# Feed-forward with features on partitions, and one group of small products for each expert

## The chip, the cores and the metric

The kernel runs on one core of a Trainium2 chip. The metric is the device time of one execution in microseconds, the median over several runs. TensorE is called PE here, VectorE DVE, ScalarE ACT, GpSimd POOL, SyncE SP, as in the profile.

## The reference

Two blocks of two layers each follow each other on 256 tokens of 1024 features, all in float32.

```python
# first block, for each of 2 layers
x = x + 0.5 * swiglu(rms_norm(x, ffn1_norm[l]), ffn1_w_gate[l], ffn1_w_up[l], ffn1_w_down[l])
x = x + mixing(rms_norm(x, mix_norm[l]))          # three kinds of attention, w_in, w_out
x = x + 0.5 * swiglu(rms_norm(x, ffn2_norm[l]), ffn2_w_gate[l], ffn2_w_up[l], ffn2_w_down[l])

def swiglu(x, w_gate, w_up, w_down):              # 1024 x 2816, 1024 x 2816, 2816 x 1024
    return (jax.nn.silu(x @ w_gate) * (x @ w_up)) @ w_down

# second block, for each of 2 layers
x = layer_norm(alpha * x + gated_linear_attention_and_sgu(x))
x = layer_norm(alpha * x + attention_to_memory(x, mem))
x = layer_norm(alpha * x + grouped_moe(x))

# grouped_moe: a router picks 2 experts of one group of 4 for each token
for e in range(16):
    h = jax.nn.silu(xt @ w_gate[e]) * (xt @ w_up[e])   # 1024 x 512 each
    y = y + gate[:, e:e + 1] * (h @ w_down[e])         # 512 x 1024
```

## The kernel before

**Weights.** All weights pass once through SBUF in units of 512 KB (`UNIT`, 128 partitions x 1024 floats), in the order of use. `load_ahead` (L261) issues their loads on SP's queue as soon as one of a number of rooms is free. Products that need full precision split each unit into a high and a low part: `whi` on ACT (L310), `wlo` on DVE (L284), and `mm3` (L356) makes three matmuls of one product, high by high, low by high, high by low. The experts take their units whole, in plain float32.

**Feed-forward.** `gated` (L515) goes through the 2816 features in the chunks of `CUTS`, of 512 and once of 256. In a chunk, `into` multiplies the 256 tokens, as two stationary tiles of 128 (`NH` halves h, tiles `xt`), with the gate weights that stream past them (bank `mm`), then with the up weights (bank `tp`); DVE makes the product (L609). Between the two stands the down product of the chunk before it (`accA`, `accB`). Down needs features on partitions, so PE turns the product in 128 x 128 transposes (L558, with `ident`), two units behind the start of the next chunk's gate, and ACT and DVE split it (L561, L562). `last_down` finishes one token half after the other, and as each of the four banks is done, `renew` adds it to `x` (L633), and the next stage's `xt` is made: transposes on PE (`transpose4`, L432), high part on ACT (L443), low part on DVE (L445), a square on ACT (L462) for the norm.

**Between.** The constants of the mixing stage are made in steps that `gated` calls at the start of chunks; their small products take banks of the kind `mm` (L169, L697, L714).

**Experts.** Each expert has 64 places. Four experts are gathered at once: `gather(q)` multiplies the tokens `xn` with the 0/1 matrix `pick` (L1834, 4 steps of 8 matmuls into a bank `tp`, copied to `xg`). `into(e)` (L1925) multiplies 64 gathered rows with gate and up, the two at once in the two column halves of the array; `turn(e)` transposes the result (L1939), ACT and DVE make the product (L1941, L1942), `down(e)` (L1950) multiplies with the down weights. `way_back(e)` turns the gated places (L1856, from `pk`, which POOL makes at L1851), and `scatter(e)` (L1966) adds the result to the tokens' banks `ys`, with 64 rows of the array. The order is written out: behind the first of `into(e + 1)`'s four pairs of units stands `turn(e)`, behind the third `scatter(e - 1)`; `way_back(e + 1)` and the steps of a gather are generators that count ticks. There are three banks `mm` and one `tp`.

**Memory.** In layer 0 the experts' stage also loads and turns the memory's tokens for layer 1 (`stage`, L1354).

Of the kernel before, what the change touches and what calls it, by code (L numbers as in the profile page):

```python
# [45 lines left out]
CUTS = [512, 256, 512, 512, 512, 512]  # L46
# [23 lines left out]
def the_kernel(  # L70
# [90 lines left out]
    def columns(c0, n, pool, *loads):  # L161

        rows = pool.tile([n, P], FT, name=f"rows{c0}") if pool else t2()[:n, :P]
        for r0, f0, t in loads:
            nc.sync.dma_start(rows[r0:r0 + t.shape[0], f0:f0 + t.shape[1]], t)

        def put():
            pt = bank("mm")[:, :n]
# [95 lines left out]
    def load_ahead(upto=None):  # L264
# [250 lines left out]
    def gated(xt, ready, chunks, scale, factor, last=True, renew=None, between={}, up="tp"):  # L515
# [3 lines left out]
        ys = []  # L519

        def into(tag, halves, hooks, done):
            W = Taken()
            o = [bank(tag)[:, :W.n] for _ in range(NH)]
            if halves == "start":

# [13 lines left out]
            order = [(h, u) for h in range(NH) for u in range(W.count)] if halves else \  # L539
                [(h, u) for u in range(W.count) for h in range(NH)]  # L540
            for i, (h, u) in enumerate(order):
                for k in W.ks(u):
                    mm3(o[h], *xt.at(h, k), *W(k), k == 0, k == KD - 1)
                if h:
                    W.close(1)
                if u == W.count - 1:
                    done(h, o[h])
                tick()
                for at, f in hooks:
                    if at == i + 1:  # L550
                        f()

        def turned(h, u, n):

            tp = tbank()
            nf = n // P
            for f in range(nf):
                nc.tensor.transpose(tp[:, f], u[:, f * P:(f + 1) * P], ident)  # L558
            uh = t2(FR).rearrange("p (f t) -> p f t", t=P)
            ul = t2(FR).rearrange("p (f t) -> p f t", t=P)  # L560
            nc.scalar.activation(uh[:, :nf], tp[:, :nf], AF.Copy)  # L561
            nc.vector.tensor_sub(ul[:, :nf], tp[:, :nf], uh[:, :nf].bitcast(FT))  # L562
            return uh, ul

        def down(c, ut):
            W = Taken()
            if not ys:
                ys.extend([bank(ACC[h]) for _ in range(2)] for h in range(NH))
            for f in range(W.kt):
                for h in range(NH):  # L570
                    for j in range(2):
                        mm3(ys[h][j], *(t[:, f] for t in ut[h]), *W(f, j), c == 0 and f == 0, False)
# [4 lines left out]
        def last_down(c, ut, gs):  # L577
            W = Taken()
            if not ys:
                ys.extend([bank(ACC[h]) for _ in range(2)] for h in range(NH))  # L580
            for h in range(NH):
                for j in range(2):
                    for f in range(W.kt):
                        mm3(ys[h][j], *(t[:, f] for t in ut[h]), *W(f, j), c == 0 and f == 0, last and f == W.kt - 1)
                        if (h, j) == (1, 1):
                            W.close(1)
                        if h == j == 0 and f == 1:
                            ut[1] = turned(1, late[1], late[2])
                        if f == W.kt - 1 and renew:
                            gs[h].append(spawn(renew(h, j, ys[h][j])))  # L590
                        if f % 2:
                            tick()

        ut, u, gs, late = {}, [None, None], [[], []], [None] * 3
        for c in range(chunks):
            if c in between:
                between[c]()
            hooks = []
            if c:
                n0 = u[0].shape[-1]  # L600
                hooks = [(2, lambda: ut.update({h: turned(h, u[h], n0) for h in range(NH)}))]
            ss = [None, None]

            def silu(h, o):
                ss[h] = t2()[:, :o.shape[-1]]
                nc.scalar.activation(ss[h], o, AF.Silu, scale=scale(h))

            def product(h, o):
                nc.vector.scalar_tensor_tensor(ss[h], o, factor(h), ss[h], op0=OP.mult, op1=OP.mult)  # L609

            into("mm", "start" if c == 0 else None, hooks, silu)
            n = ss[0].shape[-1]
            if c:
                down(c - 1, ut)
                ut = {}

            if c < chunks - 1:
                into(up, None, [], product)
            else:
                cnt = 8 * n // UNIT  # L620
                into(up, "up", [(cnt + max(1, cnt // 2), lambda: ut.update({0: turned(0, ss[0], n)}))], product)
                late[1:] = [ss[1], n]
            u = ss
        last_down(chunks - 1, ut, gs)
        return ys, gs

    def ffn(xt, rs, ready, start, between={}):

        nxt = start()
        r = lambda h: rs[h][:, 0:1]  # L630
# [1480 lines left out]
```

## Time and profile before

| | us |
|---|---|
| median of 3 runs (lowest, highest) | 2193.13 (2188.81, 2196.97) |
| profiled execution | 2191.49 |
| its span | 2189.8 |
| PE busy in the span | 2117.0 (97%) |
| DVE, ACT, POOL busy | 1118.9, 892.4, 172.5 |
| mean DMA rate | 224 GB/s |

The span goes from the first to the last instruction; the profiled execution has 1.7 us around it. Four feed-forwards take about 204, 204, 190 and 205 us, two mixing stages 221 and 217, the second block's layers about 510 and 430, of which the experts' stages take 282 (from 1478 to 1760, with the memory's keys at their end) and 224. The ends of a matmul are modelled, so that the times from one start to the next are what counts for a stream of them. TensorE's granted clock is 0.995 of full in the mean.

### The profile page before, as it was taken

How to read it: one execution, taken by the hardware profiler on the slowest of the kernel's cores; microseconds unless marked ns; L12 is line 12 of the kernel's file. 1: busy time of each engine (PE TensorE's matmuls, PEld its weight loads, DVE VectorE, ACT ScalarE, POOL GpSimd, SP SyncE). 2: the span in 40 equal slices, each digit the busy share in tenths (PEclk: the TensorE clock that was granted, in tenths of full speed). 3: DMA queues.
4: the chain of work that ended last, by engine and by line, in shares of the span. 5: the costliest groups of instructions: out<-in, count | busy, mean ns of one | idle time of the engine just before them, and what ended most of it. 6: DMA issues, size and time to landing. Idle time of an engine off the chain costs nothing. (4 is left out here: it accounts for less than half of the span.)

```text
span 2189.8 us, 29392 instructions
## 1 busy us (share of the span) xinstructions
PE 2117.0 (97%) x11117; PEld 1554.0 (71%) x11117; DVE 1118.9 (51%) x1999; ACT 892.4 (41%) x1424; POOL 172.5 (8%) x231
## 2 busy tenths in 40 slices
PE   8999999999999999999999999989999999989997
PEld 6778878788888888787888887963333677953332
DVE  6445787554555547866554547651111558341112
ACT  5444555454444446554544454521111454421111
POOL 1000100100000002102000002011000111010000
PEclk9999999999999999999999999999999999999999
DMA  7554643556556655535756555679998936589996
GB/s 250 187 181 149 211 145 111 178 177 200 174 172 193 196 159 171 187 98 173 242 183 190 158 170 198 207 258 338 393 394 297 360 116 236 178 313 383 394 393 247
DMA packets 240076, 490.48 MB, mean 224 GB/s; under 512 B 17539, under 2 KB 44851, under 8 KB 239923
## 3 DMA queue, kind: packets, MB, share of 16 engines
q1 hardware_dynamic: 239634, 487.42, 65.9%
q8 instruction: 92, 1.51, 0.3%
q10 hardware_dynamic: 288, 1.05, 0.1%
q14 instruction: 62, 0.50, 0.1%
HBM read 487.34 MB, written 1.07 MB: 223 GB/s over the span
## 5 line engine op out<-in xcount | busy, mean ns | idle before, releaser
L284 DVE TENSOR_TENSOR wlo<-raw,whi 128x1024 fp32r<-128x1024 f32 (+1 forms) x508 | 614.7, 1228 | 292.7 <-ACT whi L310 288.3
L310 ACT ACTIVATE whi<-raw 128x1024 fp32r<-128x1024 f32 (+1 forms) x508 | 525.1, 1052 | 293.3 <-PE tp L359 115.7
L1925 PE MATMUL mm<-raw,xg 128*64 128x512 f32 x1024 | 243.7, 604 | 7.7 <-PEq L1981 7.0
L357 PE MATMUL accB<-whi,xt 128*128 128x512 f32 (+3 forms) x448 | 176.2, 393 | 0.0
L359 PE MATMUL accB<-whi,xt 128*128 128x512 f32 (+3 forms) x448 | 165.5, 369 | 0.0
L358 PE MATMUL accB<-wlo,xt 128*128 128x512 f32 (+3 forms) x448 | 165.3, 369 | 0.0
L1925 PEld LDWEIGHTS mm<-raw,xg 128*64 128x64 f32 x1024 | 69.8, 137 | 133.5 <-issue 123.0
L357 PE MATMUL tp<-whi,xt 128*128 128x512 f32 (+1 forms) x384 | 143.8, 374 | 0.0
L359 PE MATMUL tp<-whi,xt 128*128 128x512 f32 (+1 forms) x384 | 143.4, 373 | 0.0
L358 PE MATMUL tp<-wlo,xt 128*128 128x512 f32 (+1 forms) x384 | 142.5, 371 | 0.0
L357 PE MATMUL mm<-whi,xt 128*128 128x512 f32 (+1 forms) x320 | 121.2, 379 | 1.4 <-DVE nbias L715 0.7
L359 PE MATMUL mm<-whi,xt 128*128 128x512 f32 (+1 forms) x320 | 118.3, 370 | 0.0
L358 PE MATMUL mm<-wlo,xt 128*128 128x512 f32 (+1 forms) x320 | 117.6, 368 | 0.0
L1950 PE MATMUL mm<-raw,t 128*64 128x512 f32 x512 | 117.3, 599 | 0.0
L1930 ACT ACTIVATE t<-mm 128x512 f32<-128x512 f32 x32 | 19.1, 597 | 188.4 <-PE mm L1925 188.4
L359 PEld LDWEIGHTS accB<-whi,xt 128*128 128x128 f32 x448 | 84.1, 188 | 15.1
L357 PEld LDWEIGHTS accB<-whi,xt 128*128 128x128 f32 x448 | 84.5, 189 | 13.3 <-issue 1.0
L358 PEld LDWEIGHTS accB<-wlo,xt 128*128 128x128 f32 x448 | 84.5, 189 | 11.6
L1859 DVE TENSOR_SCALAR back<-tp 128x256 fp32r<-128x256 f32 x32 | 13.6, 425 | 149.2 <-PE tp L1856 149.2
L609 DVE SCALAR_TENSOR_TENSOR t<-tp,ss,t 128x512 f32<-128x512 f32 (+1 forms) x48 | 33.8, 704 | 104.9 <-PE tp L359 104.9
L359 PEld LDWEIGHTS tp<-whi,xt 128*128 128x128 f32 x384 | 72.1, 188 | 13.5
L358 PEld LDWEIGHTS tp<-wlo,xt 128*128 128x128 f32 x384 | 72.1, 188 | 13.4
(515 smaller groups left out, 3950.2 us busy)
## 6 DMA issues: line engine op xcount, KB each, us to landing
raw<-in_w_gate_dram SPq DMA_DIRECT2D x128, 512.0 KB
raw<-in_w_up_dram SPq DMA_DIRECT2D x128, 512.0 KB
raw<-in_w_down_dram SPq DMA_DIRECT2D x128, 512.0 KB
raw<-in_w_in_dram SPq DMA_DIRECT2D x120, 512.0 KB
raw<-in_ffn_w_gate_dram SPq DMA_DIRECT2D x88, 512.0 KB
raw<-in_ffn_w_up_dram SPq DMA_DIRECT2D x88, 512.0 KB
raw<-in_ffn_w_down_dram SPq DMA_DIRECT2D x88, 512.0 KB
raw<-in_w_out_dram SPq DMA_DIRECT2D x32, 512.0 KB
```

What stands on the lines that cost most here:

```text
L284: eng.tensor_sub(lo, r, hi.bitcast(FT))
L310: nc.scalar.activation(hi, r, AF.Copy)
L357: nc.tensor.matmul(o, xh, wh, start=first, stop=False)
L358: nc.tensor.matmul(o, xh, wl, start=False, stop=False)
L359: nc.tensor.matmul(o, xl, wh, start=False, stop=last)
L609: nc.vector.scalar_tensor_tensor(ss[h], o, factor(h), ss[h], op0=OP.mult, op1=OP.mult)
L1859: nc.vector.tensor_scalar(bk, tp, 0.0, None, op0=OP.is_gt)
L1925: nc.tensor.matmul(p[half(i)], xgs[e // 4][k // 4][:, k % 4, e % 4], W.whole(k, i), start=k == 0, stop=k == KD - 1)
L1930: nc.scalar.activation(c[e], p, AF.Copy)
L1950: nc.tensor.matmul(p[half(j)], uu[e][:, f], W.whole(f)[:, j * 512:(j + 1) * 512], start=f == 0, stop=f == 3)
```

## The change

1. `CUTS` becomes one chunk of 512 and nine of 256. From chunk 1 on (`into_turned`), the gate and up weights are the stationary tiles of 128 features and all 256 tokens stream past them, so the result has features on partitions and is not transposed. The factors of the norm then differ along the row: `roots`, made once in a feed-forward by two small matmuls, multiplies the gate result on DVE ahead of the Silu; the up factor moves into the update of x (L667). Chunk 0 keeps its form and is still turned. In the last chunk the first 128 features are finished ahead of the second.
2. `last_down` goes through both token halves together.
3. Units that are used whole and have more than one row block are loaded so that a partition's rows lie next to each other: gate and up of the experts come in rows of 4 KB in place of 2 KB. The features of `xn` are written interleaved to match.
4. In the experts, `turn(e)`, `way_back(e + 1)`, `scatter(e - 1)` and one step of a gather stand together behind the second pair of units of `into(e + 1)`. There are two banks `mm` and two `tp`, three `back` tiles in place of two, and the rooms of odd gathers are held throughout.
5. The small products of the mixing constants and the first of the memory go to banks `tp`, and the constants are spread over one more chunk.

```diff
-CUTS = [512, 256, 512, 512, 512, 512]
+CUTS = [512] + 9 * [256]
...
-            w, c0, n, k0, m, _, _ = units[len(loads)]
+            w, c0, n, k0, m, _, whole = units[len(loads)]
             r = block(at, [UNIT], name="raw")[:, :m * n].rearrange("p (k n) -> p k n", n=n)
-            nc.sync.dma_start(r, w[k0 * P:(k0 + m) * P, c0:c0 + n].rearrange("(k p) n -> p k n", p=P))
+            if whole is True and m > 1:
+                nc.sync.dma_start(r, w[:, c0:c0 + n].rearrange("(p k) n -> p k n", p=P)[:, k0:k0 + m])
+            else:
+                nc.sync.dma_start(r, w[k0 * P:(k0 + m) * P, c0:c0 + n].rearrange("(k p) n -> p k n", p=P))
...
+        def into_turned(tag, done, hook=None, in_turn=False):
+            W = Taken()
+            o = [bank(tag)[:, :S] for _ in range(2)]
+            for fs in ((0,), (1,)) if in_turn else ((0, 1),):
+                for u in range(W.count):
+                    for k in W.ks(u):
+                        xh, xl = xt.both(k)
+                        for f in fs:
+                            wh, wl = (t[:, f * P:(f + 1) * P] for t in W(k))
+                            mm3(o[f], wh, wl, xh, xl, k == 0, k == KD - 1)
+                            if k == KD - 1:
+                                done(f, o[f])
...
+        def parts(u, to):
+            nc.scalar.activation(to[0], u, AF.Copy)
+            nc.vector.tensor_sub(to[1], u, to[0].bitcast(FT))
+            return to
...
+            gs = [[], []]
+            for i, (h, j, f) in enumerate(((0, 0, 0), (0, 1, 0), (1, 0, 0), (0, 0, 1), (0, 1, 1), (1, 0, 1), (1, 1, 0),
+                                           (1, 1, 1))):
+                mm3(ys[h][j], *at(ut, h, f), *W(f, j), False, f == 1)
+                if f:
+                    gs[h].append(spawn(renew(h, j, ys[h][j])))
...
+            if c == 1:
+                p = bank("tp")[:, :S]
+                for h in range(NH):
+                    nc.tensor.matmul(p[:, h * P:(h + 1) * P], rs[h][:, 0:1].to_broadcast([P, P]), ident, start=True,
+                                     stop=True)
+                roots.append(pool.tile([P, S], FT, name="roots"))
+                nc.vector.tensor_copy(roots[0], p)
+            def silu_turned(f, o):
+                if f == 0:
+                    silus[0] = t2()
+                nc.vector.tensor_mul(silus[0][:, f * S:(f + 1) * S], o, roots[0])
+                if f:
+                    nc.scalar.activation(silus[0], silus[0], AF.Silu)
+
+            def product_turned(f, o):
+                v = silus[0][:, f * S:(f + 1) * S]
+                nc.vector.tensor_mul(v, o, v)
+                if f == 0:
+                    silus[1:] = [t2(FR), t2(FR)]
+                if c < chunks - 1 and f:
+                    parts(silus[0], silus[1:])
+                elif c == chunks - 1:
+                    parts(v, [t[:, f * S:(f + 1) * S] for t in silus[1:]])
...
+            into_turned("mm", silu_turned, hook)
             if c in between:
                 between[c]()
...
+            down(c - 1, (True, before) if c == 1 else ut)
+            into_turned("tp", product_turned, in_turn=c == chunks - 1)
+            ut = False, silus[1:]
+        return last_down(ut)
...
-                    pn = bank("mm")
+                    pn = bank("tp")
...
-            hold(4)
+            hold(6)
...
-        xg_rooms, xn_rooms = [], take(4, 4)
+        xg_rooms, xn_rooms = take(2, 2), take(4, 4)
...
-                    nc.scalar.activation(xn[0][h][:, j * 512:(j + 1) * 512], x[h][j], AF.Copy)
+                    nc.scalar.activation(eighths(xn[0][h], j), x[h][j].rearrange("p (m k) -> p k m", k=KD), AF.Copy)
...
-            turns.enter_context(banks(mm=3, tp=1))
+            turns.enter_context(banks(mm=2, tp=2))
...
-                wt = spawn(way_back(e + 1))
-                into(e + 1, {0: lambda: turn(e), 2: lambda: e and scatter(e - 1)})
-                finish(wt)
+                pk = gated_places(e + 1)
+
+                def between():
+
+                    turn(e)
+                    way_back(e + 1, pk)
+                    if e:
+                        scatter(e - 1)
+                    next(rest_of, None)
+
+                into(e + 1, {1: between})
                 down(e, (lambda: turn(15)) if e == 14 else None)
```

How the instructions move, at three places (in these rows `t` are scratch tiles, `x_77` and `x_78` the two token halves of x). PE in layer 1's experts, before, in an expert with a gather, from `turn` to `way_back`:

```order
L1939 MATMUL tp<-ident,t_23778 128x128 x4
L1834 MATMUL tp<-pick,xn 128x256 x8
L1925 MATMUL mm<-raw,xg 64x512 x4
L1834 MATMUL tp<-pick,xn 128x256 x8
L1925 MATMUL mm<-raw,xg 64x512 x4
L1966 MATMUL accA<-t_23806,back 128x512 x2
L1966 MATMUL accA<-t_23807,back 128x512 x2
L1966 MATMUL accB<-t_23806,back 128x512 x2
L1966 MATMUL accB<-t_23807,back 128x512 x2
L1834 MATMUL tp<-pick,xn 128x256 x16
L1925 MATMUL mm<-raw,xg 64x512 x4
L1856 MATMUL tp<-ident,pk 128x128 x2
```

And PE in layer 1's experts after, one expert with a step of a gather:

```order
L1964 MATMUL mm<-raw,xg 64x512 x8
L1978 MATMUL tp<-ident,t_25536 128x128 x4
L1896 MATMUL tp<-ident,pk 128x128 x2
L2005 MATMUL accA<-t_25557,back 128x512 x2
L2005 MATMUL accA<-t_25558,back 128x512 x2
L2005 MATMUL accB<-t_25557,back 128x512 x2
L2005 MATMUL accB<-t_25558,back 128x512 x2
L1871 MATMUL tp<-pick,xn 128x256 x8
L1964 MATMUL mm<-raw,xg 64x512 x8
L1989 MATMUL mm<-raw,t_25590 64x512 x8
```

The small products, in four places there between pieces of the long one, stand in one here, and the two halves of the long one are equal. PE in the gate product of a feed-forward's chunk, before:

```order
L357 MATMUL mm<-whi,xt 128x512
L358 MATMUL mm<-wlo,xt 128x512
L359 MATMUL mm<-whi,xt 128x512
L558 MATMUL tp<-ident,t_947 128x128 x4
L558 MATMUL tp<-ident,t_956 128x128 x4
L357 MATMUL mm<-whi,xt 128x512
```

PE after, from the gate product of a chunk to the down product of the chunk before it (the two rows between are constants):

```order
L361 MATMUL mm<-xt,whi 128x256
L362 MATMUL mm<-xt,whi 128x256
L363 MATMUL mm<-xt,wlo 128x256
L169 MATMUL tp<-ident,rows_474 128x56
L744 MATMUL tp<-ident,pr 128x32
L361 MATMUL accA<-whi,t_819 128x512
```

The transposes are gone from the middle of the gate product, and its matmuls have 256 columns. DVE at the end of the first feed-forward, before:

```order
L284 TENSOR_TENSOR wlo<-raw,whi 128x1024
L633 SCALAR_TENSOR_TENSOR x_77<-accA,x_77 128x512 x2
L445 SCALAR_TENSOR_TENSOR xt<-tp,col,xt 128x128 x4
L633 SCALAR_TENSOR_TENSOR x_78<-accB,x_78 128x512
L445 SCALAR_TENSOR_TENSOR xt<-tp,col,xt 128x128 x4
```

and after:

```order
L288 TENSOR_TENSOR wlo<-raw,whi 128x1024
L667 SCALAR_TENSOR_TENSOR x_77<-accA,ss,x_77 128x512
L288 TENSOR_TENSOR wlo<-raw,whi 128x1024
L667 SCALAR_TENSOR_TENSOR x_77<-accA,ss,x_77 128x512
L667 SCALAR_TENSOR_TENSOR x_78<-accB,ss,x_78 128x512 x2
L449 SCALAR_TENSOR_TENSOR xt<-tp,col,xt 128x128 x12
```

All four updates of x now stand ahead of the first low part of `xt`, with one weight split between them.

## Rows read from the trace of the kernel before

**Rows 1.** Stages: length, busy PE, PEld, DVE, ACT, POOL, PE clock, DMA share, GB/s.

```profile
9.00:213.00 204.00, 200.84 (x923) 162.82 (x924) 111.28 (x142) 91.68 (x120) 8.41 (x20) 1.00 0.61 192
...
1478.00:1668.00 190.00, 183.94 (x904) 70.68 (x902) 30.52 (x63) 24.60 (x44) 17.28 (x30) 0.99 0.94 351
1668.00:1712.00 44.00, 39.49 (x182) 14.19 (x184) 8.56 (x16) 7.38 (x13) 1.19 (x2) 1.00 1.03 393
...
1951.00:2175.00 224.00, 217.91 (x1074) 82.95 (x1076) 36.32 (x75) 29.71 (x54) 18.85 (x32) 1.00 0.98 368
```

**Rows 2.** Timeline of PE in the first feed-forward: start, duration, instruction.

```profile
37.46 0.28 PE L357 MATMUL mm<-whi,xt 128*128 128x256 f32 x1
...
40.19 1.04 PE L558 MATMUL tp<-ident,t 128*128 128x128 f32 x8
40.98 0.36 PE L357 MATMUL mm<-whi,xt 128*128 128x256 f32 x1
41.18 0.28 PE L358 MATMUL mm<-wlo,xt 128*128 128x256 f32 x1
...
43.89 0.39 PE L357 MATMUL accA<-whi,t 128*128 128x512 f32 x1
...
46.86 0.39 PE L358 MATMUL accA<-wlo,t 128*128 128x512 f32 x1
```

**Rows 3.** Timeline at the end of the first feed-forward.

```profile
209.35 0.69 DVE L633 SCALAR_TENSOR_TENSOR x<-accB,x 128x512 f32<-128x512 f32 x1 [1.46 <-PE accB L359]
...
214.19 2.35 DVE L284 TENSOR_TENSOR wlo<-raw,whi 128x1024 fp32r<-128x1024 f32 x2
```

**Rows 4.** Waits of PE, 9 to 1250: us in total, times, longest.

```profile
PE tp L432 <- DVE x L633: 1.9, 5, 0.4
...
PE mm L357 <- DVE nbias L715: 0.7, 3, 0.2
```

**Rows 5.** Chain that ended last, layer 1's experts, one with a gather: start, us.

```profile
1971.16 1.72 PE mm L1925 x8
...
1977.60 1.13 PE tp L1834 x8
...
1990.60 1.72 PE mm L1925 x8
```

**Rows 6.** The same chain, an expert without a gather.

```profile
2035.57 1.72 PE mm L1925 x8
2037.29 0.59 PE tp L1939 x4
...
2041.46 0.67 PE accA L1966 x4
...
2042.59 1.87 PE mm L1925 x8
2044.46 0.37 PE tp L1856 x2
2044.83 3.58 PE mm L1950 x16
2048.41 1.72 PE mm L1925 x8
```

**Rows 7.** Waits in layer 1's experts, 1951 to 2175.

```profile
PE tp L1834 <- DVE t L1942: 2.9, 3, 1.1
...
PE tp L1856 <- DVE t L1942: 1.1, 1, 1.1
```

**Rows 8.** Short stretches of layer 1's experts, columns as in rows 1.

```profile
2037.50:2040.00 2.50, 2.50 (x14) 0.91 (x14) 0.42 (x1) 0.38 (x1) 0.00 (x0) 1.00 1.04 381
...
2042.50:2045.00 2.50, 2.50 (x14) 0.89 (x14) 0.13 (x1) 0.47 (x1) 0.07 (x1) 1.00 1.03 411
...
2163.00:2175.00 12.00, 12.00 (x60) 4.09 (x58) 1.93 (x4) 1.78 (x4) 0.00 (x0) 1.00 0.27 107
```

**Rows 9.** Waits of SP's queue, 1600 to 1760.

```profile
SPq L272 <- DMA stage<-in_mem_dram: 19.5, 2, 19.2
```

More of the change, by code (lines that the diff above doesn't have):

```diff
@@ L512, in first_norm, with gated, into @@
         return xt, rs
-    def gated(xt, ready, chunks, scale, factor, last=True, renew=None, between={}, up="tp"):
-        ys = []
-        def into(tag, halves, hooks, done):
+    def gated(pool, xt, ready, chunks, rs, renew, between):
+        ys = [[bank(ACC[h]) for _ in range(2)] for h in range(NH)]
+        def into(tag, done, ordered):
             W = Taken()
             o = [bank(tag)[:, :W.n] for _ in range(NH)]
-            if halves == "start":
+            if ordered:
                 for i, parts in enumerate(((0, 0), (0, 1), (1, 0))):
@@ L538, in into @@
                 return
[L539 to L563, printed above, removed]
+            for u in range(W.count):
+                for h in range(NH):
+                    for k in W.ks(u):
+                        mm3(o[h], *xt.at(h, k), *W(k), k == 0, k == KD - 1)
+                    if h:
+                        W.close(1)
+                    if u == W.count - 1:
+                        done(h, o[h])
+                    tick()
@@ new lines, in parts, with turned, at @@
+        def parts(u, to):
+            nc.scalar.activation(to[0], u, AF.Copy)
+            nc.vector.tensor_sub(to[1], u, to[0].bitcast(FT))
+            return to
+        def turned(h, u):
+            tp = transpose4(lambda f: u[:, f * P:(f + 1) * P])
+            return parts(tp, [t2(FR).rearrange("p (f t) -> p f t", t=P) for _ in range(2)])
+        def at(ut, h, f):
+            by_tokens, t = ut
+            if by_tokens:
+                return [v[:, f] for v in t[h]]
+            return [v[:, f * S + h * P:f * S + (h + 1) * P] for v in t]
@@ L575, in down, with last_down @@
                     tick()
-        def last_down(c, ut, gs):
+        def last_down(ut):
             W = Taken()
[L579 to L592, printed above, removed]
@@ new lines, in last_down, with silu, product @@
+            W.close()
+            return gs
+        ss, roots, silus = [None, None], [], [None]
+        ut = None
+        for c in range(chunks):
+            if c == 0:
+                def silu(h, o):
+                    ss[h] = t2()
+                    nc.scalar.activation(ss[h], o, AF.Silu, scale=rs[h][:, 0:1])
+                def product(h, o):
+                    nc.vector.tensor_mul(ss[h], o, ss[h])
+                into("mm", silu, True)
+                into("tp", product, False)
+                continue
+            if c == 1:
+                p = bank("tp")[:, :S]
+                for h in range(NH):
+                    nc.tensor.matmul(p[:, h * P:(h + 1) * P], rs[h][:, 0:1].to_broadcast([P, P]), ident, start=True,
[17 more added lines that the diff above has]
+                    parts(v, [t[:, f * S:(f + 1) * S] for t in silus[1:]])
+            before = {}
+            hook = (lambda: before.update({h: turned(h, ss[h]) for h in range(NH)})) if c == 1 else None
+            into_turned("mm", silu_turned, hook)
@@ L611, in gated @@
[L611 to L624, printed above, removed]
@@ L636, in ffn @@
-        return (*nxt[:-1], gs)
+            return nxt[-1](h, j, lambda xs: nc.vector.scalar_tensor_tensor(xs, y, rs[h][:, 1:2], xs, op0=OP.mult,
+                                                                          op1=OP.add))
+        with tc.tile_pool(name="ffn", bufs=1, reuse_waits="tile") as pool:
+            return (*nxt[:-1], gated(pool, xt, ready, len(CUTS), rs, renew, between))
     def mixing_constants(fb, tmp):
@@ L704, in distances, with positions @@
             nc.vector.tensor_scalar(nsink, nsink, -1.0, None, op0=OP.mult)
-            pp = bank("mm")
+        def positions():
+            for put in puts:
+                put()
+            pp = bank("tp")
             nc.tensor.transpose(pp[:, :32], pr, ident[:32, :32])
@@ L1842, in gather, with gated_places @@
                         nc.scalar.activation(o, p, AF.Copy)
-                    yield from wait(2 if q else 0)
                 if q == 3:
                     give(xn_rooms)
-            def way_back(e):
+                yield
+            def gated_places(e):
                 pk = mp.tile([P, NH, 2, CAP], FT, name="pk", bufs=2)
@@ L1852, in way_back @@
                                             gates[:, h, e:e + 1], None, op0=OP.mult)
-                yield from wait(WB)
+                return pk
+            def way_back(e, pk):
                 tp = tbank()[:, :2]
@@ L1985, in moe @@
                     slow_expert(e, rest)
-            spawn(way_back(0))
-            into(0)
+            pk = gated_places(0)
+            rest_of = gather(1)
+            next(rest_of)
+            into(0, {1: lambda: (way_back(0, pk), next(rest_of))})
             for e in range(16):
-                if e in (0, 6):
-                    hold(2)
-                if e in (7, 15):
+                if e == 15:
                     give(xg_rooms)
-                    xg_rooms.clear()
-                if e in (1, 4, 8):
-                    gs.append(spawn(gather(len(gs))))
+                if e in (3, 7):
+                    rest_of = gather(e // 4 + 2)
+                    next(rest_of)
                 if e == ME[0] and l == 0:
@@ L2064, in the_kernel @@
             memT = new_memory(4)
-            parts = memory(memT[0], "mm", 2)
+            parts = memory(memT[0], "tp", 2)
             step = lambda: next(parts, None)
```

54 lines of the change are left out of this document (21 added, 33 removed).

## The prediction

> **What bounds the kernel now.** I read the table of stages first. TensorE (PE) is busy in nearly all of each: 200.84 of 204 us in the first feed-forward, 183.94 of 190 in layer 0's experts, 217.91 of 224 in layer 1's [rows 1]. So time is won or lost in what PE itself does, at two places: the start-to-start times of its instructions in the feed-forward, read from the timeline, and the short groups between the experts' long products, read from the chain that ended last. The second column to read is the DMA share: 0.61 in the feed-forward, 0.94 to 1.03 in the experts [rows 1]. The feed-forward has bandwidth to spare. The experts live on weights loaded earlier, and in layer 0 that stock is gone for a stretch: from 1668 to 1712 the DMA engines are full at 393 GB/s while PE is busy for only 39.49 of 44 us [rows 1]. A PE saving there is worth only what the DMA can follow.
>
> **Feed-forward, the products.** Gate and up change from 512 features moving past a token tile to 256 tokens moving past a feature tile. Columns stay the same. By the order listing 1536 matmuls of 512 columns become 3072 of 256. Chunk 1 of the kernel before already runs 256 columns: 41.18 to 43.89 is 23 starts, 117.8 ns each, and then 43.89 to 46.86 is 13 starts of 512 columns, 228.5 ns each [rows 2]. A pair costs 2 x 117.8 - 228.5 = 7.1 ns more, times 1536 is **+10.9 us**. The same chunk also has 24 starts from 37.46 to 40.19, 113.75 ns each [rows 2], by which it would be -1.0 ns a pair, -1.5 us. I take the upper end: the run with 512-column work of the same stretch right behind it is the one that stands where most of the new chunks will, between two down products. The Trainium skill (TensorE: Matmul & The Clock Gate, Back-to-back issue gap) gives N/2.4 plus about 2.5 ns for the start-to-start time of one matmul, by which splitting costs 2.5 ns a pair and this term would be +3.8 us; neither of the two stretches agrees with it exactly.
>
> **Feed-forward, the transposes.** The product no longer has to be turned, except chunk 0's. Per feed-forward 44 transposes become 8: of four groups of 8 and three of 4, one of 8 stays. A group of 8 takes 40.19 to 40.98, and the matmul behind it needs 0.20 us to the next start instead of 0.12 [rows 2], so 0.87; a group of 4 is half of 0.79 plus the same 0.08, 0.48. Removed: 3 x 0.87 + 3 x 0.48 = 4.05. Added: two small matmuls that spread the norm factors over partitions, with one wait, about 0.4. Net -3.65, four times: **-14.6 us**. The new multiplications and the two-part split of the product lie on VectorE and ScalarE, under the 5.5 to 5.6 us of PE work (24 x 228.5 or 48 x 117.8 ns) between a chunk's up and the down that needs it. Gate and up rows shrink from 2 KB to 1 KB; at a DMA share of 0.61 I cost that at nothing.
>
> **Feed-forward, the end.** The last down now goes through both token halves at once, so the first half's update of x, which used to come a whole half's products ahead of the end, comes with the others. Four updates of 0.69 each follow each other on VectorE, by the order listing with one weight split of 1.2 among them (two take 2.35) [rows 3], and x must be updated before PE turns it, and its low part formed before PE uses it. Before, PE waited 1.9 us in five places for this [rows 4], at most 0.5 a feed-forward. Counting from the end of the first finished bank, VectorE ends the last update near 4.2 us, PE is ready for the last transposes near 4.0: a wait of 0.3 us, plus about 1 where the next stage takes all high parts first, since ScalarE makes those one token half behind the other. I take +1 each, **+4 us**; bounds 0 and +3 each.
>
> **Constants.** Their small products leave the banks that gate waits for: the 0.7-us wait [rows 4] goes, **-0.7 us**.
>
> **Experts.** Weight products use 64 columns of the array, the small ones 128 columns or 64 rows. The chain shows the price of coming back: x8 of L1925 takes 1.72 us behind the down product and 1.87 behind a small group, x16 of L1950 takes 3.58, which is 2 x 1.72 + 0.14 [rows 6]. So a return costs 0.145. Entering costs as well: two transposes take 0.37, four 0.59 [rows 6], which is 0.11 each and 0.15 to enter. Before, an expert has three visits; after, one: turn, way_back, scatter, and a gather step behind them. Saved: two returns and one entry, 0.44, by 15 experts, 6.6 us a layer. An expert with a gather lasts 1971.16 to 1990.60, 19.44, against 2035.57 to 2048.41, 12.84 [rows 5, 6]: 6.6 us for one gather. After, it is four steps in four visits, each 1.13 as the step that waits for nothing [rows 5], 4.5 in all. Saved 2.1, three times, 6.3 us a layer. What goes is waiting for the single turning bank [rows 7]; now there are two banks, and way_back and scatter, 0.22 + 1.1 us, cover the 1.0 that the first of them is held. The first such wait, 1.1 us [rows 7], goes too. Together 14.0 us a layer, if weights are there.
>
> Are they? In layer 1 the DMA engines are full on the mean of the stage (0.98) [rows 1] and busy for only 0.27 of the 12 us after 2163, while PE works up to 2175 [rows 8]: 12 x 0.73, some 9 us in hand, less than the 14 that PE gains. But gate and up rows become 4 KB. While gate and up land the rate is 381, in the bursts that I read as down's 4-KB rows 411 [rows 8]. The 128 units of 0.524 MB of a layer would take 163 instead of 176 us: 13 us less. In hand 9 + 13 - 14 = 8, less 2.7 for two buffers that gathered tokens now hold throughout (two units at 1.36): covered. Layer 1: **-14**. In layer 0 the queue that issues weight loads stands for 19.2 us behind the load of the memory [rows 9], and then DMA is the limit; the gain there is no more than the stream's own, of which I count what lands after the start of the stage, about 10.5: **-10.5**, bounds -5 and -14.
>
> The features are written in another interleave ahead of the gathers: as many ScalarE and VectorE instructions, strided; at most one 0.7-us instruction a layer is exposed, taken as nothing.
>
> **Sum.** 10.9 - 14.6 + 4 - 0.7 - 14 - 10.5 = -24.9 us. The profiled execution took 2191.5 us, 2189.8 of it span, so 2166.6; the median of the runs shown is 1.6 above it, which gives **2168 us**.
>
> **Rivals.**
> - *256 columns at 113.75 ns.* For it: the 24 starts of [rows 2], and those are the first of their chunk, as all are now. Against it: the longer later stretch. The first term becomes -1.5, the time 2156.
> - *The experts become bound by the DMA.* The 4-KB gain is read from bursts whose rows I only infer. Without it, and with two buffers fewer, layer 1 keeps 9 - 2.7 = 6.3 of 14 and layer 0, already empty, nothing: the sum is -24.9 + 7.7 + 10.5 = -6.7, about 2186. For it: full DMA from 1668 to 1712. Against it: the clear steps between 381 and 411. The Trainium skill (DMA: Bandwidth & Descriptors, Specifications) names about 358 GB/s as what HBM gives a core; rows of 393 and 411 stand against it as a ceiling, by which this rival would hold in full.
> - *The visits aren't cheaper.* If the array pays for each change between turn, scatter and gather what it pays for a return, the 6.6 a layer vanish: about 2180.
> - *Slower: the feed-forward's chain of product and split.* Ten chunks in place of six make 36 places per kernel where VectorE, in order, first waits for PE (L638, L644) with weight splits of 1.2 us queued behind it. If such a wait starves PE of split weights by 1.4 us a place, +50 us come on, about 2218; from 0.7 us a place the whole gain is lost. Against it: VectorE is busy for 111 of 204 us there [rows 1], and I count 1.7 us of chain under 5.5 of cover.
>
> **How the numbers follow.** Forecast 0.52, 113.75 ns 0.12, DMA 0.16, visits 0.08, slower 0.12. A measurement here can tell about 0.5%, 11 us, so faster means below 2182. The DMA case lies just above that edge, with a wide price, and I give it a quarter to faster; the visits half; the slower case leaves 0.02 within. Faster 0.52 + 0.12 + 0.04 + 0.04 = 0.72, same 0.12 + 0.04 + 0.02 = 0.18, slower 0.10. The range takes in 2156 with some for the FFN end at its best, and on the other side the DMA case with the end at its worst, +8: 2152 to 2194.
>
> **What would show it.** Layer 1's experts in about 210 us instead of 224, with one visit of 2.0 to 3.2 us an expert and PE never waiting for raw; starts of 117.8 ns in the feed-forward; waits for the update of x at each end of 0.3 to 1.5 us. DMA waits ahead of L1964 in layer 1 would show the second rival, PE idle ahead of L361 with the splits of L288 as releaser the last. A clock below full in the feed-forward would void the sum.

## The result, and the profile of the kernel after

| | before | after |
|---|---|---|
| median (lowest, highest), 4 runs each on one chip | 2190.97 (2188.58, 2196.97) | **2156.24** (2150.58, 2157.73) |
| profiled execution | 2191.49 | 2155.09 |
| its span | 2189.8 | 2153.4 |
| PE busy in the span | 2117.0 | 2088.8 |

The ratio is 0.9833, with an interval of 0.9804 to 0.9861: 35 us faster, where 25 were forecast. The time lies in the range, nearer to the rival of 113.75 ns (2156) than to the forecast (2168).

The stages of after, in the columns of [rows 1], a feed-forward first, then the experts of layer 0 and of layer 1, and 60 us out of the last:

```profile
5.00:210.00 205.00, 199.08 (x1293) 177.04 (x1292) 122.15 (x175) 93.27 (x129) 11.44 (x29) 1.00 0.64 204
...
1480.00:1660.00 180.00, 177.97 (x908) 72.98 (x908) 30.47 (x65) 25.05 (x45) 15.36 (x26) 1.00 0.99 391
...
1927.00:2138.00 211.00, 210.09 (x1072) 85.32 (x1073) 34.25 (x73) 29.58 (x53) 18.90 (x32) 1.00 1.00 396
2030.00:2090.00 60.00, 60.00 (x316) 25.15 (x312) 11.25 (x24) 8.94 (x16) 5.91 (x10) 1.00 1.03 409
```

PE is still what fills every stage: 210.09 of 211 us in layer 1's experts, with the DMA engines full beside it. To see where the time went I compare PE's first instruction of each stage in the two traces. By this much each stage changed:

| stage | before, us | after, us | change |
|---|---|---|---|
| feed-forwards, layer 0 | | | -4.4 and -0.9 |
| feed-forwards, layer 1 | | | -1.3 and -5.1 |
| experts, layer 0, with the memory's keys at their end | 279.6 | 265.4 | -14.1 |
| experts, layer 1, with the tail | 260.9 | 249.7 | -11.2 |
| all that lies between | | | about +0.6 |

(An experts' row goes from the router's first transposes to the first transposes of the next stage, so it starts earlier than the stretches of [rows 1].) So the experts gave 25.3 us, close to the forecast of 24.5, though not by the forecast's split between the layers. The feed-forwards gave 11.7 where the forecast has 0.4. The surprise is all there.

**What the feed-forward does now.** PE's timeline in a chunk, start, duration and instruction, to set against [rows 2]:

```profile
77.41 0.28 PE L361 MATMUL mm<-xt,whi 128*128 128x256 f32 x1
...
82.51 0.28 PE L361 MATMUL mm<-xt,whi 128*128 128x256 f32 x1
```

The two rows are 45 starts apart (three for each product of a stationary tile): 5.10 / 45 = 113.3 ns. All 3456 starts of 256 columns in the four feed-forwards stand in blocks of 24 with means from 113.3 to 114.5 ns, 113.6 over all. No block runs at the 117.8 of [rows 2], which the forecast took.

**What the end of a feed-forward does now.** PE at the end of the first one, then DVE in the same stretch:

```profile
203.93 0.60 PE L436 MATMUL tp<-ident,x 128*128 128x128 f32 x4
206.14 0.66 PE L436 MATMUL tp<-ident,x 128*128 128x128 f32 x4 [1.60 <-DVE xt L449]
207.17 0.66 PE L436 MATMUL tp<-ident,x 128*128 128x128 f32 x4 [0.38 <-DVE xt L449]
207.58 0.48 PE L361 MATMUL accA<-whi,xt 128*128 128x512 f32 x1
207.90 0.40 PE L362 MATMUL accA<-wlo,xt 128*128 128x512 f32 x1
```

```profile
202.99 0.75 DVE L667 SCALAR_TENSOR_TENSOR x<-accA,ss,x 128x512 f32<-128x512 f32 x1
203.65 1.40 DVE L667 SCALAR_TENSOR_TENSOR x<-accB,ss,x 128x512 f32<-128x512 f32 x2
204.96 2.15 DVE L449 SCALAR_TENSOR_TENSOR xt<-tp,col,xt 128x128 fp32r<-128x128 f32 x8
```

PE stands for 1.60 + 0.38 us, in three of the four ends, where [rows 4] has at most 0.4. The waits of PE from 5 to 1240, to set against [rows 4] (us in total, times, longest):

```profile
PE tp L436 <- DVE xt L449: 5.9, 6, 1.6
PE tp L436 <- DVE xt L444: 1.3, 1, 1.3
```

The second row is the fourth end. The releaser is not the update of x (L667), as the forecast had it, but the low part of `xt` (L449). The third quarter's x is ready at about 204.4, halfway through the pair of updates at 203.65, but PE takes it only at 206.14: the first low part has by then freed a bank. There are two banks `tp`; the first two transposes hold them until DVE has read them for the low parts; and DVE does that behind all four updates.

**The clock behind such an end.** PE at the end of the first feed-forward of layer 1, and then the granted clock (the number behind POOL) behind the ends at 207 and 816 and, between them in the rows, behind a mixing stage:

```profile
815.42 0.76 PE L436 MATMUL tp<-ident,x 128*128 128x128 f32 x4 [0.38 <-DVE xt L449]
815.83 0.77 PE L361 MATMUL accA<-whi,xt 128*128 128x512 f32 x1
816.40 0.63 PE L362 MATMUL accA<-wlo,xt 128*128 128x512 f32 x1
816.83 0.63 PE L363 MATMUL accA<-whi,xt 128*128 128x512 f32 x1
817.25 0.63 PE L361 MATMUL accA<-whi,xt 128*128 128x512 f32 x1
```

```profile
207.50:211.00 3.50, 3.50 (x18) 2.91 (x17) 2.28 (x11) 3.50 (x11) 0.56 (x1) 1.00 0.00 0
440.60:443.00 2.40, 2.40 (x9) 1.92 (x8) 2.40 (x4) 1.75 (x6) 0.00 (x0) 0.50 0.75 218
...
816.00:819.00 3.00, 3.00 (x9) 2.32 (x9) 1.95 (x10) 3.00 (x10) 0.55 (x1) 0.50 0.00 0
```

Behind the end at 207 the clock is full. Behind the one at 816 it is 0.50, the lower of its two levels, 1.2 GHz: starts of 512 columns are 427 ns apart in place of 228.5, for six to eight of them, 1.2 to 1.6 us. In this execution it happens at 441, 628, 816 and 1051, 28 slow starts in all; in the profiled one of before only at 1057, with four and part of a fifth. Only 628 and 816, with 14 of the 28, stand behind the end of a feed-forward. The other two stand behind a mixing stage, whose pause of 2.1 us before has as well.

**What an expert does now.** The chain that ended last, in layer 1's experts, the first expert and the next:

```profile
1939.12 0.60 PE tp L1978 x4
...
1939.80 0.39 ACT t L1980
1940.19 0.02 issue
1940.21 0.43 DVE t L1981
1940.65 0.04 issue
1940.69 1.20 PE tp L1871 x8
...
1952.35 0.59 PE tp L1978 x4
1952.94 0.22 PE tp L1896 x2
1953.15 0.65 PE accA L2005 x4
1953.81 0.47 PE accB L2005 x4
1954.28 1.13 PE tp L1871 x8
1955.41 3.58 PE mm L1964 x16
...
1965.86 0.59 PE tp L1978 x4
```

From the second expert on there is one visit, with nothing waited for: 0.59 + 0.22 + 0.65 + 0.47 + 1.13 = 3.06 us, and the matmuls behind it take 3.58, which pays one return. From turn to turn it is 13.51 with a step of a gather; the experts after the last step show 12.39. That is to be set against 12.84 and 19.44 in [rows 5, 6]. In the first expert `way_back` (L1896) is there, but there is no expert ahead of it to scatter, so the bank isn't covered. PE's timeline has it idle for 0.76 us there:

```profile
1939.55 0.38 PE L1896 MATMUL tp<-ident,pk 128*128 128x128 f32 x2
1940.69 1.20 PE L1871 MATMUL tp<-pick,xn 128*128 128x256 f32 x8 [0.76 <-DVE t L1981]
```

### The profile page after: what moved, and what is told of

Read it like the earlier page. It is cut to its first block, busy times and chain, and to the rows that moved or that the text cites. A ratio compares the mean times of both kernels' runs of the same rounds, so it can differ in the third digit from the quotient of the medians.

```text
span 2153.4 us, 32302 instructions
## 1 busy us (share of the span) xinstructions
PE 2088.8 (97%) x12525; PEld 1610.4 (75%) x12525; DVE 1146.6 (53%) x2107; ACT 883.3 (41%) x1420; POOL 172.9 (8%) x231
## 3 DMA queue, kind: packets, MB, share of 16 engines
HBM read 487.34 MB, written 1.07 MB: 227 GB/s over the span
## 5 line engine op out<-in xcount | busy, mean ns | idle before, releaser
L361 PE MATMUL mm<-xt,whi 128*128 128x256 f32 x576 | 159.7, 277 | 0.0
L361 PE MATMUL tp<-xt,whi 128*128 128x256 f32 x576 | 159.4, 277 | 0.0
L362 PE MATMUL tp<-xt,whi 128*128 128x256 f32 x576 | 159.3, 277 | 0.0
L363 PE MATMUL tp<-xt,wlo 128*128 128x256 f32 x576 | 159.2, 276 | 0.0
L363 PE MATMUL mm<-xt,wlo 128*128 128x256 f32 x576 | 159.1, 276 | 0.0
L362 PE MATMUL mm<-xt,whi 128*128 128x256 f32 x576 | 159.0, 276 | 0.0
L1996 DVE SCALAR_TENSOR_TENSOR t<-mm,gw,t 128x512 fp32r<-128x512 f32 x32 | 24.0, 751 | 223.2 <-ACT t L1995 223.2
L644 DVE TENSOR_TENSOR t<-tp,t 128x256 f32<-128x256 f32 x72 | 27.9, 424 | 181.3 <-PE tp L363 181.3
L1989 PE MATMUL mm<-raw,t 128*64 128x512 f32 x512 | 116.7, 594 | 1.1 <-DMA raw<-in_w_down_dram 1.0
L362 PEld LDWEIGHTS tp<-xt,whi 128*128 128x128 f32 x576 | 108.3, 188 | 1.5
L361 PEld LDWEIGHTS tp<-xt,whi 128*128 128x128 f32 x576 | 108.1, 188 | 1.5
L363 PEld LDWEIGHTS tp<-xt,wlo 128*128 128x128 f32 x576 | 108.2, 188 | 0.0
L362 PEld LDWEIGHTS mm<-xt,whi 128*128 128x128 f32 x576 | 108.2, 188 | 0.0
L361 PEld LDWEIGHTS mm<-xt,whi 128*128 128x128 f32 x576 | 108.1, 188 | 0.0
L363 PEld LDWEIGHTS mm<-xt,wlo 128*128 128x128 f32 x576 | 108.1, 188 | 0.0
```

The costliest lines, as they stand in the source:

```text
L361: nc.tensor.matmul(o, xh, wh, start=first, stop=False)
L362: nc.tensor.matmul(o, xh, wl, start=False, stop=False)
L363: nc.tensor.matmul(o, xl, wh, start=False, stop=last)
L644: nc.vector.tensor_mul(v, o, v)
L1989: nc.tensor.matmul(p[half(j)], uu[e][:, f], W.whole(f)[:, j * 512:(j + 1) * 512], start=f == 0, stop=f == 3)
L1996: nc.vector.scalar_tensor_tensor(yl, p, gw, yh.bitcast(FT), op0=OP.mult, op1=OP.subtract)
```

## The experiments

Each is read against the kernel before on the same chip; the stage times are from its profile.

**The two halves of the change, each alone.** `e1_ffn_only` has points 1, 2 and 5 of the change and the experts as before, `e2_exp_only` points 3 and 4 and the feed-forwards as before. The lines that part them, each against the kernel before, the first in e1 alone and the others in e2 alone:

```diff
-CUTS = [512, 256, 512, 512, 512, 512]
+CUTS = [512] + 9 * [256]
```

```diff
-            turns.enter_context(banks(mm=3, tp=1))
+            turns.enter_context(banks(mm=2, tp=2))
...
-                into(e + 1, {0: lambda: turn(e), 2: lambda: e and scatter(e - 1)})
+                into(e + 1, {1: between})
```

> The kernel before with the feed-forward's part of the change alone (chunks of 256 with features on partitions, the joint last down, the constants' and memory's small products in other banks); the experts stay as before. Theory (stages compared by the first matmul of the next one): the feed-forwards give 11.7 us of the 36.4 that the span lost, so about 12 us less than before, span near 2178, and starts of 113.3 to 113.8 ns in the turned chunks. Rival, the recorded sum: 117.8 ns a start, where the feed-forward part is worth 0.4 us and the time is that of before within 1 us.

> The kernel before with the experts' part alone (one visit of small products an expert, two banks to turn in, 4-KB rows, interleaved features); the feed-forward stays as before. Theory: 25 us less than before (14 in layer 0, 11 in layer 1), span near 2165, with expert periods of 12.39 us without and 13.51 with a gather step. Rival: the experts gain only because the feed-forward changed what was loaded ahead; then layer 0's experts lose some 5 us or more of it to waits for weights.

Measured: 2176.47 against 2190.73, ratio 0.9936 (0.9915 to 0.9957), for the feed-forward alone: -14.3 us. For the experts alone 2167.72, 0.9889 (0.9864 to 0.9914): -23.0. Together 37.3 where both made 34.7, so the two add up within the intervals. In e2's profile the experts' steps are those of after (13.51 and 12.38), so they don't need the changed feed-forward. The feed-forward part is worth 14 us by itself; the forecast's 0.4 is refuted. In e1's profile only the pause at 438 is followed by a low clock, with 7 slow starts where after has 28: 4 us of the difference by which its stages up to layer 0's router are 16.0 us shorter than before's, and those of after only 10.7.

**Smaller chunks in the old form.** Is the price of 117.8 ns wrong for 256 columns, or only for the form that the change brings? The kernel before with one line changed:

```diff
-CUTS = [512, 256, 512, 512, 512, 512]
+CUTS = [512] + 9 * [256]
```

> The kernel before with only the chunk sizes changed to one of 512 and nine of 256: token tiles stay stationary, the product is still turned, in groups of 4 transposes. It measures 256 columns in the old form. If the rate belongs to the form (features that stream past tokens), starts are 117.8 ns in nearly all chunks, 1536 pairs x 7 ns = 11 us, and the kernel is 11 to 16 us slower than before with the re-entries behind twice as many transposes' groups. If the rate depends on what ran ahead and not on the form, many chunks run at 113.3 ns as the changed kernel's, and it is 0 to 5 us slower.

Measured: 2201.18 against 2190.68, ratio 1.0052 (1.0033 to 1.007): +10.5 us. Its timeline of PE has both rates, each held for a whole block of 24:

```profile
62.02 0.28 PE L358 MATMUL mm<-wlo,xt 128*128 128x256 f32 x1
...
64.51 0.28 PE L359 MATMUL mm<-whi,xt 128*128 128x256 f32 x1
...
81.06 0.28 PE L358 MATMUL mm<-wlo,xt 128*128 128x256 f32 x1
...
83.66 0.28 PE L359 MATMUL mm<-whi,xt 128*128 128x256 f32 x1
```

22 starts apart each: 2.49 and 2.60 us, 113.2 and 118.2 ns a start by these rounded times. Of its 3456 starts of 256 columns, 2640 stand in blocks of 117.8 ns and 816 in blocks of 113.3. In the old form, where split weights stream past tokens, the row that the forecast took prices most of the blocks. In the new form, where tokens stream past weights, it prices none. The slower rate belongs to the old form, then, and not to the width. A start takes 116.7 ns on the mean of these blocks, a pair 4.9 ns more than 228.5, which is 7.6 us for 1536. Of the other 3 of the 10.5, some 1.6 are longer waits at the ends (1.9 us in [rows 4]):

```profile
PE tp L432 <- DVE xt L445: 3.5, 3, 1.2
```

L445 forms the low part of `xt`, so here too a transpose waits for it, though the last down product keeps its old order. Why a block of the old form takes one rate or the other stays open.

**The 4-KB rows alone undone.** The change with the experts' units in 2-KB rows and `xn` not interleaved:

```diff
-            if whole is True and m > 1:
-                nc.sync.dma_start(r, w[:, c0:c0 + n].rearrange("(p k) n -> p k n", p=P)[:, k0:k0 + m])
...
-                    nc.scalar.activation(eighths(xn[0][h], j), x[h][j].rearrange("p (m k) -> p k m", k=KD), AF.Copy)
+                    nc.scalar.activation(xn[0][h][:, j * 512:(j + 1) * 512], x[h][j], AF.Copy)
```

> The changed kernel with gate and up of the experts in rows of 2 KB again, and features not interleaved. Theory (the second rival of the prediction, had the 4-KB rows given nothing): the stream takes about 10 to 13 us longer a layer than in the changed kernel, whose last expert weights arrive only 3 us ahead of use; so PE waits for weights, 7 to 10 us in layer 1 and about as much in layer 0: 12 to 20 us slower than the changed kernel. Rival: the rate is set by the memory and not by the rows, and nothing changes beyond 1 us a layer; or the strided writes of the interleave were the larger cost, and it is up to 2 us faster.

Measured: 2163.42, ratio 0.9873 (0.9847 to 0.9898), 7.2 us above after by the medians, whose intervals overlap a little; by stages, layer 0's experts +2.9 and layer 1's +6.5. The first expert of a stage ran at half clock in after's layer 0 and in e3's layer 1, not in the other two, so it is better to count from the second expert's start to the stage's end: +5.8 and +4.8. (Of the 5.8, some may be the clock, at half from 1693 to 1704 in e3.) A stretch of layer 1's experts in its profile, and one of its waits, in layer 0 (us in total, times, longest):

```profile
2040.00:2100.00 60.00, 60.00 (x308) 24.14 (x306) 9.20 (x19) 8.56 (x15) 4.74 (x8) 1.00 1.04 393
```

```profile
PE mm L1984 <- DMA raw<-in_w_down_dram: 2.5, 5, 0.8
```

With 2-KB rows a full DMA moves 393 GB/s, with 4-KB rows 409, 4%. That is some 7 us of a 176-us stream, not the 13 that the forecast took from bursts. The experts' steps are as in after (13.51 and 12.39) until the stock of loaded weights runs out: the last two in layer 0 are 15.63 and 17.51, in after 13.68 and 16.83. So the longer rows matter, as an insurance that is drawn on at the end of a stage, and for less than their whole gain. That the DMA rival fell rests on them only in part: even without them 7 of the 25 us would be lost, not 18.

**A visit of its own for way_back.** Is the price of a visit right, 0.145 to return and 0.15 to enter [rows 6]? The change with `way_back` one pair of units later:

```diff
-                    way_back(e + 1, pk)
...
-                into(e + 1, {1: between})
+                into(e + 1, {1: between, 2: lambda: way_back(e + 1, pk)})
```

> The changed kernel with way_back taken out of the joint group and put behind the third pair of units, as a visit of its own (two 128-column transposes between long products). By the prices read from the chain, 0.15 to enter and 0.145 to return, 29 to 30 visits cost 8.9 us more; periods go from 12.39 to 12.68 and from 13.51 to 13.81. Rival: the visits weren't what was saved (the gain came from waits for the single bank), then the time is that of the changed kernel; or the larger slack of PE feeds the DMA-bound stretch of layer 0 and only layer 1's half shows, 4.5 us.

Measured: 2160.18, ratio 0.9861 (0.9836 to 0.9886), 3.9 us above after by medians, whose intervals overlap. The stages are sharper. Its chain of waits in layer 1's experts:

```profile
2000.96 1.87 PE mm L1964 x8
2002.83 0.37 PE tp L1896 x2
2003.20 1.87 PE mm L1964 x8
2005.06 3.43 PE mm L1989 x16
```

The 16 matmuls take 3.74 in place of 3.58, and the two transposes 0.37 in place of 0.22: 0.31 us, once an expert. Steps are 13.82 and 12.69 where after has 13.51 and 12.39, over 13 of them 3.9 us more in each layer. The visit's price is as forecast, and the rival that grouping saves nothing falls.

**What PE waits for at the end of a feed-forward.** Two theories: that the updates of x come too late, all four of them behind the joined last down product; or that the two banks `tp` are held. `e4_half_first` does the first token half's four products ahead of the second half's:

```diff
-            for i, (h, j, f) in enumerate(((0, 0, 0), (0, 1, 0), (1, 0, 0), (0, 0, 1), (0, 1, 1), (1, 0, 1), (1, 1, 0),
+            for i, (h, j, f) in enumerate(((0, 0, 0), (0, 1, 0), (0, 0, 1), (0, 1, 1), (1, 0, 0), (1, 0, 1), (1, 1, 0),
```

> The changed kernel with the last down product in another order: the first token half's four products first, then the second half's. Theory: the ends of the feed-forwards cost PE 2 us of idle each, and after two or three of them the granted clock is at half for some 3 us, 1.5 us more; with the first half's updates done 2.8 us earlier most of it goes: 5 to 12 us faster than the changed kernel, and the granted clock stays at 1.00 behind the ends. Rival: the second 128 features aren't split in time for the third product (1.4 us of cover instead of 2.1), PE waits there instead, and the time is the same within 2 us.

Measured: 2158.89, ratio 0.9849 (0.9825 to 0.9873), no gain. PE at the end of its first feed-forward:

```profile
203.81 0.40 PE L363 MATMUL accB<-whi,t 128*128 128x512 f32 x1
206.08 0.66 PE L436 MATMUL tp<-ident,x 128*128 128x128 f32 x4 [1.88 <-DVE xt L449]
207.11 1.12 PE L436 MATMUL tp<-ident,x 128*128 128x128 f32 x4 [0.38 <-DVE xt L449]
207.88 0.78 PE L361 MATMUL accA<-whi,xt 128*128 128x512 f32 x1
208.45 0.63 PE L362 MATMUL accA<-wlo,xt 128*128 128x512 f32 x1
```

The first half's products and updates stand earlier, and the third transpose still starts at 206.08: the wait only became longer, 1.88, though the x that it turns is ready at 203.9. The theory of the late x falls. `e5_banks` gives the second token half other banks, at the two ends that stand ahead of a mixing stage, where `mm` is free:

```diff
-        tp = transpose4(lambda k: xs[:, k * P:(k + 1) * P])
+        tp = transpose4(lambda k: xs[:, k * P:(k + 1) * P], "mm" if h and c0 in (MIXC, MIXC + 8) else "tp")
```

> The changed kernel, where the two transposes of the second token half at the end of each layer's first feed-forward go to banks of the kind mm in place of tp. Theory: PE's 2 us of idle there isn't the update of x; the third transpose waits for one of two tp banks, which VectorE frees only with the low part of xt that it forms behind all four updates. With two banks more the 1.6 us of wait at those two ends shrink to under 0.6 us, and what clock is lost behind them is not lost: 3 to 6 us faster than the changed kernel. Rival: VectorE itself is late (four updates and a weight split in a row); then the wait moves to the first matmul of the next stage, and the time is the same.

Measured: 2146.92, ratio 0.9803 (0.9781 to 0.9824). Its PE at the same end, the granted clock behind it, and what is left of the wait:

```profile
205.11 0.60 PE L436 MATMUL tp<-ident,x 128*128 128x128 f32 x4
205.63 0.55 PE L436 MATMUL mm<-ident,x 128*128 128x128 f32 x3
```

```profile
206.00:209.00 3.00, 3.00 (x17) 2.38 (x16) 2.73 (x11) 3.00 (x13) 0.00 (x0) 1.00 0.44 152
```

```profile
PE tp L436 <- DVE xt L449: 2.0, 2, 1.6
```

The wait is gone where the banks were given, and still stands at the end of layer 0's second feed-forward, where they were not. So the cause is the bank. (The fourth end keeps its wait for L444, 1.2 us in e5; it was not tested.) `e6_banks_half` has both edits:

> The same two banks, and the first token half's down products ahead of the second half's. Theory of the banks: 1 us an end better than the other banks alone, since the updates of the first half also come earlier: 4 to 8 us faster than the changed kernel. Rival as there: VectorE's order decides, and the time is that of the order alone (2.6 us slower than the changed kernel) or of the changed kernel.

Measured: 2149.45, ratio 0.9816 (0.9794 to 0.9838): nothing more than e5.

Since e5 ran on another chip than after, the two were set side by side on one:

> The changed kernel as it is, beside the kernel with two more turning banks (e9_after_again and e10_banks_again stand on one chip, so that the two are compared without a change of chip). Expected: 0.983 of the kernel before, some 2155 us, with PE idle 1.6 + 0.4 us behind the last down product of both feed-forwards ahead of a mixing stage, and the granted clock at half behind some of the ends.

> The second token half is transposed into banks mm at the end of the two feed-forwards ahead of a mixing stage, the rest as in the changed kernel. Theory that the wait is for a turning bank: the two waits of 2.0 us go, 4 us, and with them the drops of the granted clock that stand behind them, 0 to 3 us by the execution: 4 to 7 us less than e9_after_again. Rival, that the gain between two chips was chance: no difference within 2 us.

Measured: 2154.1 (2150.95 to 2156.93) and 2146.41 (2144.86 to 2150.15), ratios 0.9831 (0.9809 to 0.9853) and 0.98 (0.9778 to 0.9822). The slowest run with the banks is faster than the fastest without: 7.7 us, of which 4 are the two waits. The rest fits the clock, but isn't shown to be the clock alone: at the two ends that lost their pause it is full in the profiles of e5 and e10, and in e9's it is at half behind both (208 and 816). It is also at half behind a mixing stage in e9 (443) and not in e10, where both kernels have the same pause of 2.1 us. Of the kernel before, the changed one and the one with the banks, the last is the fastest, 44 to 45 us below the kernel before.

## Why the prediction held, and where it didn't

| term | forecast | measured, and from what |
|---|---|---|
| products | +10.9 | about -2: 1536 x (2 x 113.6 - 228.5 ns) |
| transposes | -14.6 | not measured alone; some -16 is left of the 10.7 us that PE has gained at layer 0's router |
| ends of the feed-forwards | +4 | about +8: waits of 7.2 us in place of 1.9, and 14 slow starts of 0.2 |
| clock behind the mixing stages | not in the sum | about +2: 14 slow starts where before has four |
| constants | -0.7 | about -2.8 |
| experts, layer 1 | -14 | -11.2 |
| experts, layer 0 | -10.5 | -14.1 |

**Products: the step that failed.** The rows showed two rates for the same width, and I took the one that "stands where most of the new chunks will". In the new form the place made no difference. Both rows were of the old form, so neither was a row of the new one, and the 7.1 ns a pair belonged in the bounds. The difference, 13 us, is more than the whole miss of 12. The rival of 113.75 ns, with a chance of 0.12, was the right case, and it should have had about as much as the forecast. The Trainium skill (TensorE: Matmul & The Clock Gate, Back-to-back issue gap) gives N/2.4 + 2.5 ns for the gap of a single matmul, from which 109.2 ns is an estimate for 256 columns; no block in any run here is faster than 113.3.

**Ends: right in sign, wrong in mechanism, and half the size.** The forecast followed the updates of x along DVE and found 0.3 us of wait for x. It left out who else needs DVE there: a bank `tp` comes free only when its low parts are made, and these queue behind the updates. e4 and e5 show it. The smaller part of the cost, the clock behind the pauses, was named only as something that would void the sum.

**Constants: mis-sized.** Only the wait of 0.7 us [rows 4] was counted. But the group of four matmuls of L714, now at L751, takes 1.31 us up to the next product where it took 2.11 with that wait in it, three times, 2.4 us; with some 0.4 at the smaller products the first feed-forward gains about 2.8.

**Experts: the mechanism and its prices held.** One visit in place of three was to save 0.44 and saves 0.45 (12.84 to 12.39). A step of a gather was to cost 1.13 and costs 1.12 (13.51 less 12.39). From the second expert's start to the last one's, layer 1 went from 186.4 to 172.4 us: -14.0, the forecast itself. Of this 2.9 came back ahead of it: 1.3 ahead of the first expert's weights, 1.6 in the first expert, which now holds a gather step and still has the wait that the forecast had gone. I had counted way_back and scatter as cover there, but the first expert has no scatter. The interleaved write of `xn` takes DVE 1.07 us in place of 0.68, but e3, without it, takes as long to the first expert's weights (23.5 us from the stage's start, after 23.4), so it isn't shown to be the cause.

**Layer 0: the forecast was too careful.** From the second expert's start to the last one's it lost 17.8 us (195.8 to 178.0), and 3.7 came back around it: 2.0 in the first expert and 3.1 behind the last one's start, less 1.4 ahead of the first. Why, I did not take apart. The bound, "no more than the stream's own", assumed that PE lives on arriving weights through the whole stage. It does so only in the last two experts. They take 30.5 us in after and 35.0 in before, so here the faster stream pays, and the eleven steps ahead of them pay in full.

**The other rivals.** The slower feed-forward chain of product and split did not appear: PE is busy for 199.08 of 205 us there, and no wait for a split of 0.5 us or more stands ahead of its turned products. The range held, for a partly wrong reason: 13 us too much for the products were set off in part by 4 too little for the ends and 2 for the clock behind the mixing stages. That the experts' sum came out within 1 us is partly luck too: layer 1 gave 2.8 less than forecast, layer 0 gave 3.6 more.

## What to carry to other kernels

A row prices an instruction only in its own form: where two rows of the same width disagree and the new code swaps what streams and what stands, both ends belong into the bounds, and the choice between them into the rivals with like chances. Where several results are turned through few banks, follow the bank to its last reader: here the low part, queued behind four updates on the same engine, and not the data, set the pause, and two idle banks took it away at the two ends that got them. Group small products by what they cost to enter and to leave, measured in the chain; that price held to 0.02 us.

## What the chip showed that was not expected

- One form and width of matmul runs at either of two steady rates, 113.3 or 117.8 ns a start for 256 columns, for a block of 24 or 48 at a time. With tokens streaming every block of after was near the faster (113.3 to 114.5 on the mean), with weights streaming (e7) a quarter of the starts. Neither which banks alternate (the last chunk of after finishes one half before the other, at the same rate) nor the width tells them apart.
- A pause of PE of 1.6 to 2.1 us behind a feed-forward or a mixing stage costs up to 1.6 us more than itself, since the granted clock can be at half behind it. In the 12 profiles it was so behind 26 of 45 such pauses, in kernels old and new; the same pause of the same kernel shows it in one execution and not in another (207 in after has 1.00; in e9 the clock there is at half).
